# Sums of weight blocks made in DRAM: another order of copies and additions, and another place for a part of them

## The chip, the core and the metric

The kernel runs on one core of a Trainium2 chip. The core has five engines, each with an instruction queue of its own: PE (TensorE, matrix products; its weight loads are listed apart as PEld), DVE (VectorE), ACT (ScalarE), POOL (GpSimd) and SP (SyncE, which here only issues DMAs). DMAs are issued from the queues of SP, ACT and POOL. The metric is device time of the whole program in microseconds (us); lower is better. Times of several runs and one profiled execution are given.

## The reference

One inference step of a two-layer streaming encoder, for a prompt of 512 tokens and a running stream of 64 more, 576 columns in all, width 1024. Each layer is a token mixer (layer 0: causal pooling; layer 1: sparse attention with a rotary embedding, an indexer that picks 256 keys per token, and cached keys and values for the running stream) and a squared-ReLU MLP of width 4096, with residual adds and RMS norms:

```python
def _mlp(h, w_up, w_down):
    u = jax.nn.relu(h @ w_up)
    return (u * u) @ w_down

for i in range(DEPTH):
    h = _rmsnorm(x, norm_mix[i])
    ...
    x = x + y.astype(x.dtype)
    x = x + _mlp(_rmsnorm(x, norm_mlp[i]), mlp_w_up[i], mlp_w_down[i]).astype(x.dtype)
```

## The kernel before

**Products.** Activations lie transposed in SBUF, 128 features by 576 tokens. Every f32 weight block is split in two parts, an upper one that ACT casts (line 207) and a lower one, the difference that DVE or POOL makes (line 208), and PE multiplies three combinations. A weight block of 128 x 1024 is loaded into a tile `raw` by SP (the MLPs) or ACT (the attention), line 146. Blocks are made two ahead of PE (`next_block`).

**Fewer products.** Where two row blocks and two token halves meet, `Pair` (`DownPair`, `UpPair`) computes a 2 x 2 block product with seven products instead of eight (Strassen's scheme in Winograd's form). Besides the weights themselves it needs four sums of the weights' quarters a11, a12, a21, a22: s1 = a21 + a22, s3 = a21 + a11, s2 = s1 + a11, s4 = s2 + a12 (signs are taken care of elsewhere). In layer 0 the down products are pairs, and their sums are made in SBUF by POOL (lines 258 to 263, tile `sum`), from weights that SP loads. In layer 1 there are 24 pairs (12 up, 12 down), and their sums are made in DRAM ahead of time, in a tensor `mixed`: for each sum SP copies the first term into its place (line 218, 256 KB), and POOL then issues a DMA that adds the second term there (line 220). In the second MLP, SP loads `raw<-mixed` like any weight. So for one pair there are four copies and four additions, with a chain s1, s2, s4.

**Order.** `mixing` is a generator that issues a copy, yields, issues its addition, yields: eight steps a pair, pair after pair. In the first MLP each of the 16 calls of `up` takes seven steps (14 pairs, 56 sums), in the second each of the first 16 pairs takes five (10 pairs, 40 sums). A copy is placed behind the latest weight load of SP (`issue_after`). A scheduler then orders the instructions of each engine; the engine executes them in that order, so that whatever waits holds what stands behind it.

**The late attention.** `steps` runs over 40 units (one key group, two heads or a part of the running stream): scores on PE, softmax on DVE and ACT (line 1204), transposes, values, and from unit 18 on the output projection of the first 256 tokens (`wa`). Group by group, four units ahead, SP loads the queries (line 1279), and for the last four groups the cached keys (line 1084), which ACT casts and POOL subtracts (lines 286 and 287). POOL also makes index scores (lines 1171 and 1173) until the units of line 1225 with 384 columns begin.

Of the kernel before, what the change touches and what calls it, by code (L numbers as in the profile page):

```python
# [12 lines left out]
ALU = mybir.AluOpType  # L13
# [3 lines left out]
P = 128  # L17
# [26 lines left out]
AHEAD = 2  # L44
BLOCKS = 3
VS = 2
MIXES = (7, 5)


@with_exitstack  # L50
def pool_dsa_kernel(ctx: ExitStack, tc: tile.TileContext, a, o):
# [56 lines left out]
    def f32(t):  # L108
        return t.bitcast(F32)
# [100 lines left out]

    def mixing():

        for (kind, c, q), n in pairs.items():
            (a11, a12), (a21, a22) = ([r[:, i * 512:(i + 1) * 512] for i in range(2)] for r in rows(kind, 1, c, q))
            s1, s2, s3, s4 = (mixed[:, n, i] for i in range(4))
            for dst, src, add in ((s1, a21, a22), (s3, a21, a11), (s2, s1, a11), (s4, s2, a12)):
                with tc.issue_after(last_of["sync"].ins):
                    nc.sync.dma_start(dst, src)
                yield
                pool.dma_start(dst, add, accum_op=ALU.add)  # L220
                yield

    mixes = mixing()
# [259 lines left out]
    def mlp(layer, gi, strassen, order=range(KT), end=None):  # L483
# [165 lines left out]

        bx0 = norm.s2[:, :HT]  # L650

        def mix():
            for _ in range(MIXES[layer]):
                next(mixes, None)

        def up(c, q):
            if not layer:
                mix()
            if q >= PLAIN[layer][c]:
                mix()  # L660
                v = new_v()
                pair = UpPair(bx, seeded(), v)
                pair.opening()
                pair.closing()
                activated(v)
                finished(c, q, v)
                return
            first = (c, q) == (0, 0)
            pts = []
            if not layer and not first and not late:  # L670
                v = new_v()
                for i in range(2):
                    pt = up_plain(range(KT))
                    for h in range(2):
                        dve.scalar_tensor_tensor(v[:, 2 * i + h], pt[h][:, :HT], 0.0, halves(norm.rb)[:, h], ALU.max, ALU.mult)
                    act.activation(v[:, 2 * i:2 * i + 2], v[:, 2 * i:2 * i + 2], AF.Square)
                    if (c, q) == (3, 3):
                        us[c][q] = us[c][q] or u_tile()
                        factors_by_tile(i, v, us[c][q])
                if us[c][q] is None or q == 0:  # L680
                    finished(c, q, v)
                return
            for i in range(2):
                pts.append(up_plain(order if first else range(KT)))
                if late:
                    norm.spread()
                    v = new_v()
                    activated(v, late.pop())
                    finished(c, 0, v)
                if not first:  # L690
                    with tc.issue_after(last_of["diag"].ins), tc.issue_after(last_of["rt"].ins):
                        next(mixed, None)
            if first:
                norm.stats()
                late.append(pts)
                return
            v = new_v()
            activated(v, pts)
            finished(c, q, v)
# [4 lines left out]
        for c in range(4):  # L704
            for q in range(c > 0, 4):
                up(c, q)
            if c < 3:
                up(c + 1, 0)
            if c < strassen:
                for q in range(KT // 2):  # L710
                    if layer:
                        mix()
                    pair = DownPair(q, us[c], seeded(), layer > 0)
                    pair.opening(c == 3 and q == 0)
                    pair.closing((c, q) != (3, 3))
                continue
            phase["spare"] = room("bx", 7, "spare")[:7]
            for m in range(KT if end is None or c < 3 else KT - LAST):
                w = next_block()
                pt = [psum1("dn") for _ in range(2)]  # L720
                project(tuple(pt), w, us[c])
                for h in range(2):
                    d = halves(x[m])[:, h]
                    dve.tensor_tensor(d, d, pt[h][:, :HT], ALU.add)
# [302 lines left out]
    def attention(parts):  # L1027
# [244 lines left out]
        class Group:  # L1272
            def __init__(self, i, g):
# [2 lines left out]
                self.sums = small(n, f"sums{n}")  # L1276
                if i < 4:
                    self.q = slot("a", "q")[:, :4 * P].rearrange("p (h t) -> p h t", h=4)
                    nc.sync.dma_start(f32(self.q), qd[g][:, :, i * P:(i + 1) * P])
                else:  # L1280
                    self.q = slot("a", "q")[:, :4 * TS].rearrange("p (j t) -> p j t", j=2)
                    for j in range(2):
                        nc.sync.dma_start(f32(self.q[:, j].rearrange("p (h t) -> p h t", h=2)), qd[g][:, j::2, TP:T])
                    self.ck = split_cache(a["cache_k"][g], "ck", ks[g], pool)

            def normalise(self):
# [43 lines left out]
        def steps():  # L1330

            ranked = {0}
            for u in range(-4, total + 2):
# [18 lines left out]
                    units[u - 2].group.outputs()  # L1352
                if u >= 18 and u % 2 == 0:
                    next(first_out, None)
                yield

        def pace():
# [152 lines left out]
```

## Time and profile before

| | us |
|---|---|
| runs | 1166.62 median of 3 (1161.0 to 1167.46) |
| the profiled execution | 1167.88, its span 1166.0 |
| before and in the first MLP | 0 to 455 |
| first half of the attention, to the last index score on POOL | 455 to 619 |
| late attention and output projection | 619 to 741 |
| second MLP and end | 741 to 1166 |
| PE busy, share of the span | 1097.8 (94%) |

A row of the table of stretches has, for each engine, busy time and (x) instructions, then the granted TensorE clock, the share of time in which the 16 DMA engines were busy, and GB/s. A row of a timeline has start, length, engine, line, operation, out<-in, count, and in brackets the idle time before it and what ended it. SPq and POOLq are the queues of the engines that issue DMAs.

### The profile page before, as it was taken

Reading aid. Unit: us, or ns where it says so; the run is one execution under the profiler, and the core shown is the slowest. Engines: PE = TensorE matmul, PEld = TensorE weight load, DVE = VectorE, ACT = ScalarE, POOL = GpSimd, SP = SyncE. Lnnn points to the kernel's source line nnn. Section 1 sums busy time; section 2 is a strip of 40 time slices with the busy share of each in tenths; the row PEclk is TensorE's granted clock in tenths of the full one; section 3 lists DMA queues with packets and bytes.
Section 4 is the critical chain, followed back from the end, with each engine's and each line's share of the span. In section 5 each row is a group of like instructions: output and inputs, shape, how many; then the busy total and the mean of one; then the engine's idle time right before and its main releaser. Section 6 shows DMA issues by size and latency. Waiting matters only on the chain.

```text
span 1166.0 us, 20650 instructions
## 1 busy us (share of the span) xinstructions
PE 1097.8 (94%) x8118; PEld 1078.4 (92%) x8118; DVE 791.0 (68%) x1438; ACT 555.6 (48%) x925; POOL 310.8 (27%) x275
## 2 busy tenths in 40 slices
PE   8999999899789999999899999999999699899995
PEld 8998999899789999999889999999998699899995
DVE  7766657556556777659999944798657566765644
ACT  8443334334234445435388665566346335544531
POOL 3224423422441540047963440000111111000002
PEclk9999999999989999999989999999999899999998
DMA  6867368547735745357642341536888888745402
GB/s 215 191 180 149 94 186 194 112 141 174 161 91 153 179 127 179 107 136 212 182 125 65 116 142 48 172 104 179 231 237 245 220 225 254 216 137 177 140 19 82
DMA packets 81745, 183.54 MB, mean 157 GB/s; under 512 B 12289, under 2 KB 23856, under 8 KB 81648
## 3 DMA queue, kind: packets, MB, share of 16 engines
q1 hardware_dynamic: 63072, 139.71, 38.0%
q0 software_dynamic: 13824, 25.17, 14.2%
q10 hardware_dynamic: 4752, 17.34, 4.9%
q8 instruction: 64, 1.05, 0.4%
q14 instruction: 33, 0.27, 0.1%
HBM read 167.10 MB, written 61.22 MB: 196 GB/s over the span
## 4 chain that ended last, share of the span: by engine, by line
PE 46%; DVE 11%; DMA 9%; ACT 3%; issue 2%; POOL 1%; SPq 0%; DVEq 0%; ACTq 0%; POOLq 0%
PE seed L403 8%; PE up L557 6%; PE c L403 5%; PE a L403 5%; PE dn L300 4%; DMA mixed<-in_w_down 4%; PE pj L300 4%; DVE w L208 3%; PE o L1264 3%; PE wo L300 2%; PE wa L300 2%; DMA raw<-mixed 2%; DVE work L1189 2%; PE sc L1225 2%; DVE m L1188 1%
## 5 line engine op out<-in xcount | busy, mean ns | idle before, releaser
L207 ACT CAST w<-raw 128x1024 fp32r<-128x1024 f32 (+2 forms) x242 | 211.6, 889 | 274.8 <-PE seed L403 81.4
L208 DVE TENSOR_TENSOR w<-raw,w 128x1024 fp32r<-128x1024 f32 (+2 forms) x224 | 243.8, 1095 | 105.3 <-ACT w L207 104.2
L557 PE MATMUL up<-xs,w 128*128 128x288 f32 x1536 | 205.9, 295 | 0.5 <-ACT rbm L331 0.5
L557 PEld LDWEIGHTS up<-xs,w 128*128 128x128 f32 x1536 | 203.8, 188 | 0.9 <-ACT rbm L331 0.9
L403 PE MATMUL seed<-u,w 128*128 128x288 f32 x1008 | 150.2, 300 | 19.7 <-ACT seed L428 19.3
L403 PEld LDWEIGHTS seed<-u,w 128*128 128x128 f32 x1008 | 141.3, 192 | 21.7 <-ACT seed L428 21.1
L403 PE MATMUL a<-u,w 128*128 128x288 f32 x672 | 104.5, 302 | 6.9 <-ACT w L207 5.6
L220 POOL DMA_DIRECT2D mixed<-in_w_up x48 | 39.6, 851 | 259.2 <-DMA mixed<-mixed 140.4
L403 PE MATMUL c<-u,w 128*128 128x288 f32 x672 | 102.7, 298 | 3.0 <-ACT u L592 1.9
L403 PEld LDWEIGHTS a<-u,w 128*128 128x128 f32 x672 | 96.3, 194 | 8.5 <-ACT w L207 6.0
L403 PEld LDWEIGHTS c<-u,w 128*128 128x128 f32 x672 | 94.5, 190 | 4.4 <-ACT u L592 2.2
L300 PE MATMUL pj<-xs,w 128*128 128x288 f32 x672 | 93.0, 294 | 0.0
L220 POOL DMA_DIRECT2D mixed<-in_w_down x48 | 40.2, 894 | 192.0 <-DMA mixed<-mixed 155.9
L300 PEld LDWEIGHTS pj<-xs,w 128*128 128x128 f32 x672 | 90.5, 188 | 0.7
L403 PE MATMUL seed<-bx,w 128*128 128x288 f32 x432 | 65.7, 305 | 6.2 <-ACT seed L428 6.2
L208 DVE TENSOR_TENSOR w<-sum,w 128x1024 fp32r<-128x1024 f32 (+1 forms) x32 | 33.8, 1056 | 51.8 <-ACT w L207 51.6
L403 PEld LDWEIGHTS seed<-bx,w 128*128 128x128 f32 x432 | 61.7, 195 | 7.0 <-ACT seed L428 6.9
L207 ACT CAST w<-sum 128x1024 fp32r<-128x1024 f32 (+1 forms) x32 | 26.7, 834 | 72.4 <-POOL sum L263 63.4
L300 PE MATMUL dn<-u,w 128*128 128x288 f32 (+2 forms) x384 | 51.9, 295 | 1.0 <-ACT u L286 1.0
L300 PEld LDWEIGHTS dn<-u,w 128*128 128x128 f32 x384 | 51.0, 188 | 1.4 <-ACT u L286 1.2
L754 POOL TENSOR_TENSOR x<-x,spare 128x320 f32<-128x320 f32 (+1 forms) x9 | 8.1, 934 | 148.4 <-ACT spare L750 148.4
L1204 ACT ACTIVATE p<-p,nm 128x128 f32<-128x128 f32 (+4 forms) x72 | 41.9, 583 | 11.7 <-DVE nm L1203 11.1
(279 smaller groups left out, 1934.9 us busy)
## 6 DMA issues: line engine op xcount, KB each, us to landing
raw<-in_w_up SPq DMA_DIRECT2D x52, 512.0 KB, 4.3
raw<-in_w_down SPq DMA_DIRECT2D x52, 512.0 KB, 4.2
raw<-mixed SPq DMA_DIRECT2D x48, 512.0 KB, 5.3
mixed<-in_w_down POOLq DMA_DIRECT2D x48, 256.0 KB, 6.1
mixed<-mixed SPq DMA_DIRECT2D x48, 256.0 KB, 3.3
mixed<-in_w_up POOLq DMA_DIRECT2D x48, 256.0 KB, 5.7
raw<-in_w_o ACTq DMA_DIRECT2D x16, 512.0 KB, 4.1
raw<-in_w_in ACTq DMA_DIRECT2D x15, 512.0 KB, 4.3
```

Of the source, the lines that this page charges most:

```text
L207: act.copy(w[:, 0, at], src[:, at])
L208: how["sub"].tensor_tensor(w[:, 1, at], src[:, at], f32(w[:, 0, at]), ALU.subtract)
L220: pool.dma_start(dst, add, accum_op=ALU.add)
L300: pe.matmul(pt[h][:, :m] if isinstance(pt, tuple) else pt[:, h, :m], wt, xs[k][:, part, c:c + m], start=(k == 0 and i == 0), stop=(k == n ...
L403: pe.matmul(bank[:, :HT], wt[:, at], ut, start=first and j == 0 and i == 0, stop=j == 3 and i == 2, skip_group_check=True)
L557: pe.matmul(pt[h][:, :HT], w[:, wt, k * P:(k + 1) * P], moving(k, part, h), start=n == 0 and i == 0, stop=n == KT - 1 and i == 2)
L754: pool.tensor_tensor(x[k][:, t], x[k][:, t], rb, ALU.mult)
L1188: dve.max(m8[:np_], wk[:np_])
L1189: dve.match_replace(wk[:np_], m8[:np_], wk[:np_], TAKEN)
L1204: act.activation(dst, dst, AF.Exp, scale=-1.0, bias=nm, accum_out=sums)
L1225: pe.matmul(pt[:, hh, :nw], q[:, 2 * s + hh], ks[g][:, part, :nw], start=part == 0, stop=part == 1)
L1264: pe.matmul(oc[:, 2 * s + hh], pT[:, c:c + P], V[:, kt, vs], start=kt == 0, stop=kt == i)
```

## The change

The order of the sums is changed, and where the steps are taken; the sums, their number and the products stay. `mixing` now goes over all pairs n together: a step with the copies of s1 and s3 of pair n, then a step with the copies of s2 of pair n - 1 and s4 of pair n - 2; each step first issues the additions of the step before. That makes 28 x 2 = 56 steps for 24 pairs, the last four pairs' worth of which only drain. A step is taken by every call of `up` and every down pair of the first MLP (16 + 16 = 32 steps), by the units from 18 on of the attention (u = 18 to 41, 24 steps), and by the pairs of the second MLP. 32 and 24 are all 56, so that the calls in the second MLP find nothing left, although the change was described as reaching six of its pairs. The loads of queries set `last_of["sync"]`, so that a copy in the attention is placed behind the latest of them.

```diff
-MIXES = (7, 5)
...
     def mixing():
-        for (kind, c, q), n in pairs.items():
+        def parts(p):
+            kind, c, q = order[p]
             (a11, a12), (a21, a22) = ([r[:, i * 512:(i + 1) * 512] for i in range(2)] for r in rows(kind, 1, c, q))
-            s1, s2, s3, s4 = (mixed[:, n, i] for i in range(4))
-            for dst, src, add in ((s1, a21, a22), (s3, a21, a11), (s2, s1, a11), (s4, s2, a12)):
-                with tc.issue_after(last_of["sync"].ins):
-                    nc.sync.dma_start(dst, src)
-                yield
-                pool.dma_start(dst, add, accum_op=ALU.add)
+            s1, s2, s3, s4 = (mixed[:, p, i] for i in range(4))
+            return {"s1": (s1, a21, a22), "s3": (s3, a21, a11), "s2": (s2, s1, a11), "s4": (s4, s2, a12)}
+
+        order, copied = list(pairs), []
+        for n in range(len(order) + 4):
+            for step in (((n, "s1"), (n, "s3")), ((n - 1, "s2"), (n - 2, "s4"))):
+                for dst, add in copied:
+                    pool.dma_start(dst, add, accum_op=ALU.add)
+                copied.clear()
+                for p, name in step:
+                    if 0 <= p < len(order):
+                        dst, src, add = parts(p)[name]
+                        with tc.issue_after(last_of["sync"].ins):
+                            nc.sync.dma_start(dst, src)
+                        copied.append((dst, add))
                 yield
...
-        def mix():
-            for _ in range(MIXES[layer]):
+        def up(c, q):
+            if not layer or q >= PLAIN[layer][c]:
                 next(mixes, None)
-
-        def up(c, q):
-            if not layer:
-                mix()
             if q >= PLAIN[layer][c]:
-                mix()
                 v = new_v()
...
                 for q in range(KT // 2):
-                    if layer:
-                        mix()
+                    next(mixes, None)
                     pair = DownPair(q, us[c], seeded(), layer > 0)
...
-                    nc.sync.dma_start(f32(self.q), qd[g][:, :, i * P:(i + 1) * P])
+                    last_of["sync"] = nc.sync.dma_start(f32(self.q), qd[g][:, :, i * P:(i + 1) * P])
...
                 if u >= 18 and u % 2 == 0:
                     next(first_out, None)
+                if u >= 18:
+                    next(mixes, None)
                 yield
```

The queues, as the scheduler orders them. **POOL in the first MLP**, third group of down pairs (`sum` and `raw` are the pairs' sums and weights, `mixed` the additions). Before:

```order
L258 TENSOR_TENSOR sum_3225<-raw_3015 128x512
L220 DMA mixed<-in_w_down 128x512
L259 TENSOR_TENSOR sum_3225<-sum_3225,raw_3013 128x512
L261 TENSOR_TENSOR raw_3015<-raw_3015,raw_3013 128x512
L220 DMA mixed<-in_w_down 128x512 x2
L258 TENSOR_TENSOR sum_3416<-raw_3149 128x512
L220 DMA mixed<-in_w_down 128x512
L259 TENSOR_TENSOR sum_3416<-sum_3416,raw_3147 128x512
L261 TENSOR_TENSOR raw_3149<-raw_3149,raw_3147 128x512
L220 DMA mixed<-in_w_down 128x512 x3
L263 TENSOR_TENSOR sum_3225<-sum_3225,raw_3013 128x512
L258 TENSOR_TENSOR sum_3530<-raw_3414 128x512
```

The same place after the change:

```order
L267 TENSOR_TENSOR sum_3210<-raw_3006 128x512
L222 DMA mixed<-in_w_down 128x512
L268 TENSOR_TENSOR sum_3210<-sum_3210,raw_3004 128x512
L270 TENSOR_TENSOR raw_3006<-raw_3006,raw_3004 128x512
L222 DMA mixed<-in_w_up 128x512
L267 TENSOR_TENSOR sum_3405<-raw_3137 128x512
L222 DMA mixed<-in_w_down 128x512
L268 TENSOR_TENSOR sum_3405<-sum_3405,raw_3135 128x512
L270 TENSOR_TENSOR raw_3137<-raw_3137,raw_3135 128x512
L222 DMA mixed<-in_w_down 128x512 x3
L272 TENSOR_TENSOR sum_3210<-sum_3210,raw_3004 128x512
L267 TENSOR_TENSOR sum_3523<-raw_3403 128x512
```

Three additions still stand ahead of the first pair's last sum (now line 272), but they are an s3, an s2 and an s4 of three different pairs, where before they were links of one pair's chain; and additions now also stand among the sums that follow.

**SP in the late attention**, from the last query load with 128 tokens on (`x<-xd` is the residual stream read back). Before:

```order
L1279 DMA q_7339<-q_6141 128x4x128
L1392 DMA x_8017<-xd 128x1152
L1084 DMA raw_7455<-in_cache_k 128x512
L1283 DMA q_7450<-q_5683 128x2x64 x2
L1392 DMA x_8018<-xd 128x1152
L1084 DMA raw_7572<-in_cache_k 128x512
```

After:

```order
L1282 DMA q_7379<-q_6149 128x4x128
L228 DMA mixed<-in_w_up 128x512 x2
L228 DMA mixed<-mixed 128x512
L1397 DMA x_8097<-xd 128x1152
L228 DMA mixed<-mixed 128x512
L1087 DMA raw_7503<-in_cache_k 128x512
L1286 DMA q_7498<-q_5691 128x2x64 x2
L228 DMA mixed<-in_w_up 128x512 x2
L228 DMA mixed<-mixed 128x512
L1397 DMA x_8098<-xd 128x1152
L228 DMA mixed<-mixed 128x512
L1087 DMA raw_7628<-in_cache_k 128x512
```

Ahead of each load of cached keys (line 1087) there now stand four copies, of which two (`mixed<-mixed`) wait for an addition. All 35 copies left by the first MLP stand in this part of SP's queue, 34 of them ahead of the last load of cached keys.

**SP in the second MLP**, two down pairs. Before:

```order
L146 DMA raw_9279<-in_w_down 128x1024
L146 DMA raw_9281<-mixed 128x1024
L146 DMA raw_9283<-mixed 128x1024
L218 DMA mixed<-mixed 128x512
L146 DMA raw_9285<-in_w_down 128x512
L218 DMA mixed<-in_w_down 128x512 x2
L146 DMA raw_9397<-in_w_down 128x1024
```

After:

```order
L145 DMA raw_9344<-in_w_down 128x1024
L145 DMA raw_9346<-mixed 128x1024
L145 DMA raw_9348<-mixed 128x1024
L145 DMA raw_9350<-in_w_down 128x512
L145 DMA raw_9457<-in_w_down 128x1024
```

No copy stands between the weights there any more, nor anywhere else in the second MLP.

More of the change, by code (lines that the diff above doesn't have):

```diff
@@ L1282, in __init__ @@
                     for j in range(2):
-                        nc.sync.dma_start(f32(self.q[:, j].rearrange("p (h t) -> p h t", h=2)), qd[g][:, j::2, TP:T])
+                        last_of["sync"] = nc.sync.dma_start(f32(self.q[:, j].rearrange("p (h t) -> p h t", h=2)), qd[g][:, j::2, TP:T])
                     self.ck = split_cache(a["cache_k"][g], "ck", ks[g], pool)
```

## Prediction

> **What bounds the kernel now.** I read the page first (slices), then a table of stretches, then the waits of the two MLPs, then single waits in order of time.
>
> ```profile
> PE   8999999899789999999899999999999699899995
> DMA  6867368547735745357642341536888888745402
> ```
>
> A slice is 29.15 us. PE is nearly always busy, so the time is won or lost in the few thin slices: the 11th (291 to 321 us, first MLP), the 32nd (904 to 933) and the 35th (991 to 1020, both second MLP). The DMA row is at 7 or 8 from the 29th slice to the 35th, and low, 1 to 4, in the late attention (22nd to 25th, 612 to 729 us).
>
> ```profile
> core 0: us, PE busy (x) PEld busy (x) DVE busy (x) ACT busy (x) POOL busy (x), PEclk, DMA share, GB/s
> 100.00:120.00 20.00, 17.65 (x117) 16.48 (x116) 11.01 (x16) 6.28 (x8) 7.70 (x8) 0.91 0.63 127
> 200.00:220.00 20.00, 16.56 (x116) 16.32 (x115) 11.12 (x17) 6.54 (x9) 9.66 (x8) 0.93 0.68 162
> 300.00:340.00 40.00, 28.26 (x198) 28.02 (x197) 18.71 (x27) 9.84 (x13) 18.07 (x15) 0.83 0.58 125
> 617.00:694.00 77.00, 76.77 (x636) 74.83 (x635) 62.14 (x182) 52.93 (x127) 27.83 (x25) 1.00 0.33 96
> 850.00:1010.00 160.00, 141.05 (x991) 137.83 (x990) 102.71 (x138) 77.35 (x111) 22.86 (x28) 0.95 0.85 236
> 1010.00:1030.00 20.00, 17.62 (x126) 16.69 (x125) 15.62 (x21) 10.94 (x14) 0.00 (x0) 1.00 0.51 146
> 1030.00:1100.00 70.00, 70.00 (x527) 70.00 (x526) 44.38 (x59) 34.73 (x49) 0.00 (x0) 1.00 0.55 167
> ```
>
> I count matmuls rather than busy time, because a slow matmul is busy too. Undisturbed, 527 matmuls run in 70 us: 7.53 a us. By that rate the rows before fall short by 4.5 us (117 of 150.6), 4.6, 13.7, and for 850 to 1010 by 28.4 us (991 are 131.6 us of work). The late attention, 617 to 694, has full PE and a DMA share of 0.33.
>
> Why the first MLP loses: the waits of 60 to 460 us (who waited for whom, total, times, longest), and then SP, POOL and PE in order of time:
>
> ```profile
> POOL mixed L220 <- DMA mixed<-mixed: 144.8, 20, 15.1
> ...
> ACT w L207 <- POOL sum L263: 63.4, 15, 12.8
> ```
> ```profile
> 306.49 0.48 SPq L218 DMA_DIRECT2D mixed<-mixed  x1
> ...
> 314.59 0.48 SPq L218 DMA_DIRECT2D mixed<-mixed  x1
> ```
> ```profile
> 313.08 1.93 POOL L220 DMA_DIRECT2D mixed<-in_w_down  x2
> 320.16 0.81 POOL L220 DMA_DIRECT2D mixed<-in_w_down  x1 [5.15 <-DMA mixed<-mixed]
> 320.70 1.55 POOL L263 TENSOR_TENSOR sum<-sum,raw 128x512 f32<-128x512 f32 x1
> ```
> ```profile
> 325.43 3.25 PE L403 MATMUL seed<-u,w 128*128 128x288 f32 x12 [11.74 <-ACT seed L428]
> ```
>
> POOL's additions wait for copies, a copy s2 or s4 waits on SP for the addition before it (306.49, 314.59), and sum L263, which the next weight block needs, stands on POOL behind such an addition: it runs at 320.70, and ACT had waited up to 12.8 us for it. PE then idles 11.74 us.
>
> Why the second MLP loses: SP's own waits of 850 to 1010 us, and one case on SP and PE:
>
> ```profile
> SPq L218 <- DMA mixed<-in_w_down: 45.1, 6, 9.6
> SPq L218 <- DMA mixed<-in_w_up: 41.6, 6, 9.3
> ```
> ```profile
> 913.45 0.48 SPq L218 DMA_DIRECT2D mixed<-mixed  x1
> 914.03 0.53 SPq L146 DMA_DIRECT2D raw<-in_w_down  x1
> ```
> ```profile
> 921.84 0.85 PE L403 MATMUL a<-u,w 128*128 128x288 f32 x2 [4.71 <-ACT w L207]
> ```
>
> From 850 to 1010 SP stands 86.7 of 160 us at copies that wait for additions. One case: it is held at a copy until 913.45, only then issues the weights of 914.03, and PE waits 4.71 us for the block made of them. SP's queue, not the transfer alone, is the bound there.
>
> **The change part by part.** The sum is made against the profiled execution, 1167.88 us (span 1166.0 and 1.88 around it), 1.26 us over the median 1166.62 of the runs shown.
>
> *Nothing is saved in work:* 96 copies and 96 additions before and after; the counting of steps gives 61 of each in the first MLP where 56 stood, and the last 35 in the attention instead of 40 in the second MLP. No step of it is left for the second MLP.
>
> *First MLP.* The two-hop chain ahead of L263 goes. After the change three additions still stand ahead of the sum (order below the change), but s1, s3 and s2 wait for nothing recent, and s4 only for an s2 addition issued a step earlier; that is one hop, an addition and a copy (6.1 and 3.3 us, rows below), where 306.49 to 320.16 shows two, 13.7 us. One hop less is some 9 us earlier; of the 12.8 us that ACT waited at the worst place, up to 4 remain, and PE's 11.74 idle us began about a us after ACT's, so that 3 or so can remain. At 100 and 200 us the waits were half as long and vanish. Of 4.5 + 4.6 + 13.7 = 22.8 us I take 19 back, bounds 8 (POOL is held a hop in every group) and 23. New here: two copies and two additions beside each down pair, where none stood. An addition holds POOL some 0.8 us (313.08 has two in 1.93), against sums of 1.55 us; I cost it at nothing because the pairs' sums stand two blocks ahead of PE. If that cover is gone, it is the 8.
>
> *Second MLP.* All sums are gone from SP, and the stretch 850 to 1010 becomes like 1030 to 1100, which already runs without them: full rate at a DMA share of 0.55. One loss there is no DMA: where the third chunk passes from ups to downs (1010 to 1030, no sums in flight) 126 matmuls take 20 us, 3.3 us lost, and the like will stay at the second chunk. 28.4 - 3.3 = 25 us back, bounds 18 and 28.
>
> *Late attention.* Here 35 copies and 35 additions come into a stretch that lost nothing. The queues' shares of 750 to 1010 us (packets, MB, share), the page's issues (KB each, median us to landing), and POOL, ACT and PE in order of time:
>
> ```profile
> q1 hardware_dynamic: 16154, 43.83, 50.8%
> q0 software_dynamic: 5760, 10.49, 24.8%
> ```
> ```profile
> mixed<-in_w_down POOLq DMA_DIRECT2D x48, 256.0 KB, 6.1
> mixed<-mixed SPq DMA_DIRECT2D x48, 256.0 KB, 3.3
> ```
> ```profile
> 616.35 2.90 POOL L1173 TENSOR_TENSOR work<-work,rl 64x576 f32<-64x576 f32 x2
> ```
> ```profile
> 656.45 0.62 ACT L286 CAST ck<-raw 128x512 fp32r<-128x512 f32 x1 [1.65 <-DMA raw<-in_cache_k]
> ...
> 693.52 0.62 ACT L286 CAST ck<-raw 128x512 fp32r<-128x512 f32 x1
> 694.05 0.78 ACT L1204 ACTIVATE p<-p,nm 128x576 f32<-128x576 f32 x1
> ```
> ```profile
> 703.23 0.76 PE L1233 MATMUL sc<-ck,q 128*128 128x288 f32 x4
> ```
>
> Price of a sum in time of the 16 DMA engines, from the two queue rows (750 to 1010 us, 260 us): q0 holds 40 additions (10.49 MB by 0.262), 0.248 x 260 / 40 = 1.61 us each; q1 moves a MB in 0.508 x 260 / 43.83 = 3.01 us, so a copy of 0.262 MB is 0.79 us. SP's new order puts 34 of the copies, and so 32 additions that they or their successors wait for, ahead of the load of the last cached keys (raw<-in_cache_k). They can start when POOL is done with the index scores, at 619.25 (616.35 + 2.90). Work to be done before that load lands: 32 x 1.61 + 34 x 0.79 = 78.4 us, and what the stretch moves already, 0.33 x 77 = 25.4: together 103.8 us in the 74.3 us to 693.52, where ACT casts those keys. At full engines they land at about 723, 29.5 us late. ACT's order is fixed: behind the cast stands the softmax of 694.05, and the first keys' cast at 656.45 already waited 1.65 us for its load with a softmax behind it; so a late load holds all of ACT's queue. PE needs the cast keys at 703.23, 9.7 us after the cast, and half of that is work in between (POOL's difference, the softmax); I take 5 us as slack that ACT can lose. 25 us remain, spread over the four casts of cached keys. Bounds: nothing (all hidden) and 42 (the same work at the 0.85 share of the stretch 850 to 1010: 103.8 / 0.85 = 122, landing at 741, 48 late, less 5).
>
> The Trainium skill, "DMA: Bandwidth & Descriptors", section "Anatomy of one DMA — SWDGE (gpsimd) path", fits a DMA issued by GpSimd as 2.0 us plus bytes by 436 GB/s. By it an addition of 256 KB would hold the engines an estimated 0.6 us instead of the 1.61 of the trace, the work would be 32 x 0.6 + 26.9 + 25.4 = 72 us, and it would just fit: the attention would lose nothing. The trace has the price and decides; by the page the time would be that of the first rival.
>
> *Sum:* 1167.88 - 19 - 25 + 25 = 1148.9 in the profiled execution, 1147.6 by the median. I predict 1148.
>
> **The rivals.**
>
> *The attention hides the sums.* Its DMA row is 1 to 4 tenths, PE has 5 us of slack per cast, and the engines can be seen at more than full share for a while:
>
> ```profile
> 170.00:180.00 10.00, 10.00 (x78) 10.00 (x77) 6.79 (x11) 5.30 (x6) 3.21 (x4) 1.00 1.06 278
> ```
>
> Against it stands that 1.06 over the whole stretch still makes 98 us of 74. If the price of an addition alone on its engines is much under 1.61, it holds: 1167.9 - 44, 1124 (1123 by the median). Chance 0.15.
>
> *The attention is held as the second MLP was.* SP waits for additions, POOL for copies, and the engines are filled to 0.85 only: +42 instead of +25, 1166, no change. After the idle 11.74 us at 325.43 the first 12 matmuls took 3.25 us, where 12 take 1.59 at 7.53 a us. The Trainium skill, "TensorE: Matmul & The Clock Gate", Part 1, says that the array's clock is halved after an idle window of some 3.4 us and for about as long; the trace agrees (3.25 against 1.59), and by it four stalls of that length would add an estimated 1.7 us each, 1173 in this case. Chance 0.13.
>
> *Slower.* One mechanism: ACT's in-order wait at the four casts of cached keys. It decides when it costs more than the 44 us won, that is when the last keys land after 742 (693.5 + 44 + 5), the engines being filled under 0.84; at 0.78, landing at 752, the loss is 54 and the time 1177. For it: four hops (copy, addition, copy, addition) lie between loads, and SP has nothing else to issue meanwhile. Against it: two to three pairs are in flight at once, which is what the stagger does. Chance 0.09.
>
> *The change doesn't do what it says* in the first MLP: three additions still stand ahead of the sum, the wins there are 8 and the rest as forecast: 1160. Chance 0.08; my own forecast has the remaining 0.55.
>
> **How the numbers follow.** Likeliest 1148 (0.55, with its own range 1138 to 1160). The range reaches down to 1127, almost to the hidden case, and up to 1167, past the case without change: 0.8. A measurement of this kernel tells about 0.5% from no change, 5.8 us. Faster by more than that (under 1160.8): 0.15, 0.53 of the likeliest, half of the 0.08, and 0.03 of the held case, 0.75. Within: 0.02 + 0.04 + 0.08 of the held case + 0.02 of the slower one, 0.16. Slower: the rest of those two, 0.09. The range leaves out half of the hidden case (0.07) and, above, the slower one and the upper third of the held one (0.13).
>
> **What would show it.** First MLP: waits of ACT for the sum (63.4 us before) under 20, PE's 11.74 gone or under 4. Second MLP: no wait of SP at a copy, 850 to 1010 (shifted) at 7.4 matmuls a us or more. Attention: a DMA share of 0.9 or more from 620 on, waits of ACT for raw<-in_cache_k of 20 us or more in total (1.65 at the first keys before), the second MLP's first matmul 25 us late beside what the first MLP won. Wrong would be: the attention's share full and no wait of ACT (then the cover is larger than I read), or the second MLP still thin without sums (then its weights, not the sums, were late).

## The result

The change takes 1161.82 us (median of 20 runs, 1151.22 to 1169.82), the kernel before 1167.40 (median of 20, 1160.76 to 1171.48). The ratio is 0.9942, with a 95% interval of 0.9919 to 0.9965: faster by 5.6 us, where 19 were forecast. The ratio leaves out the slowest run of after, which counts as a slow one (without it the median is 1160.86). The profiled execution of after took 1165.96 us, its span 1164.2.

The slices of the page after the change, to be laid beside those of before:

```profile
PE   9999999999999989999797897999999999999995
PEclk9999999999999999999898995999999999999997
DMA  6346686586676674456559995243455555545402
```

The thin slices of both MLPs are gone (11th, 32nd, 35th before). New thin ones stand at the 22nd, 23rd and 25th (611 to 669 and 698 to 728 us), the late attention, and the last of them has a granted clock of 5 tenths. The table of stretches says the same in counts of matmuls (columns as before):

```profile
300.00:340.00 40.00, 39.04 (x290) 38.50 (x290) 26.29 (x38) 14.90 (x19) 18.57 (x18) 1.00 0.66 153
617.00:694.00 77.00, 66.07 (x517) 63.65 (x515) 49.32 (x137) 40.51 (x93) 43.66 (x47) 0.93 1.07 263
694.00:740.00 46.00, 39.28 (x217) 36.77 (x216) 10.98 (x32) 14.53 (x41) 10.12 (x11) 0.70 0.43 110
850.00:1010.00 160.00, 157.63 (x1165) 156.70 (x1164) 116.56 (x157) 87.46 (x122) 0.00 (x0) 0.99 0.53 158
```

From 300 to 340 us PE runs 290 matmuls (198 before), from 850 to 1010 it runs 1165 (991). From 617 to 694 it runs 517 (636), with the DMA engines full, and after that at a clock of 0.70. (The attention begins 12.9 us earlier after the change, at 442.1 us, so equal times are not quite equal work there; the table below is free of that.)

To put every kernel of this study on one scale, I cut each profiled execution at four matmuls: the first of the first MLP (`up`), the first of the attention (`pj`), the last of the output projection (`wo`) and the last of the second MLP (`dn`). In us:

| | first MLP | attention | second MLP |
|---|---|---|---|
| before | 418.1 | 285.7 | 410.2 |
| after | 406.1 (-12.0) | 318.4 (+32.7) | 387.7 (-22.5) |
| forecast | -19 | +25 | -25 |

The three differences and 0.8 us ahead of the first MLP make -2.6; the end takes 0.9 us longer, and the spans differ by 1.8. These are two single executions, as is every stretch given for the kernels below. That the medians lie 5.6 apart and not 2 is the spread between runs, of which more below: the profiled run of after is 4 us above its median.

### The profile page after: what moved, and what is told of

Its sections match the earlier page's. It is cut to its first block, busy times and chain, and to the rows that moved or that the text cites. A ratio compares the mean times of both kernels' runs of the same rounds, so it can differ in the third digit from the quotient of the medians.

```text
span 1164.2 us, 20675 instructions
## 1 busy us (share of the span) xinstructions
PE 1104.6 (95%) x8118; PEld 1086.0 (93%) x8118; DVE 808.9 (69%) x1438; ACT 555.6 (48%) x925; POOL 307.4 (26%) x275
## 4 chain that ended last, share of the span: by engine, by line
PE 53%; DVE 9%; DMA 9%; issue 3%; POOL 3%; ACT 3%; SPq 0%; DVEq 0%; ACTq 0%; POOLq 0%
PE seed L412 13%; PE c L412 8%; PE up L566 8%; PE a L412 8%; PE dn L309 4%; PE pj L309 3%; DVE w L207 2%; DMA mixed<-in_w_down 2%; DMA raw<-in_cache_k 2%; DMA raw<-in_w_down 2%; PE v L1061 1%; ACT w L206 1%; DVE work L1192 1%; DMA mixed<-mixed 1%; DVE m L1191 1%
## 5 line engine op out<-in xcount | busy, mean ns | idle before, releaser
L412 PEld LDWEIGHTS seed<-u,w 128*128 128x128 f32 x1008 | 138.9, 188 | 11.9 <-ACT seed L437 5.3
L267 POOL TENSOR_TENSOR sum<-raw 128x512 f32<-128x512 f32 x16 | 24.9, 1556 | 152.7 <-DMA raw<-in_w_down 145.0
L207 DVE TENSOR_TENSOR w<-sum,w 128x1024 fp32r<-128x1024 f32 (+1 forms) x32 | 42.0, 1313 | 29.7 <-ACT w L206 29.7
L412 PE MATMUL seed<-bx,w 128*128 128x288 f32 x432 | 62.5, 296 | 0.0
L412 PEld LDWEIGHTS seed<-bx,w 128*128 128x128 f32 x432 | 59.3, 188 | 0.1
L222 POOL DMA_DIRECT2D mixed<-in_w_up x48 | 43.6, 1012 | 40.2 <-DMA mixed<-mixed 21.9
L206 ACT CAST w<-sum 128x1024 fp32r<-128x1024 f32 (+1 forms) x32 | 26.6, 833 | 48.3 <-POOL sum L272 41.1
```

What stands on the lines that cost most here:

```text
L206: act.copy(w[:, 0, at], src[:, at])
L207: how["sub"].tensor_tensor(w[:, 1, at], src[:, at], f32(w[:, 0, at]), ALU.subtract)
L267: pool.tensor_tensor(s[:, :512], r2[:, :512], r2[:, 512:], ALU.add)
L412: pe.matmul(bank[:, :HT], wt[:, at], ut, start=first and j == 0 and i == 0, stop=j == 3 and i == 2, skip_group_check=True)
```

## Where the attention's 32.7 us are

PE's idle times there, what SP, POOL and ACT waited for from 600 to 745 us (total, times, longest), and the two DMA queues from 620 to 700 us (packets, MB, share):

```profile
631.44 1.33 PE L1248 MATMUL pt<-ident,p 128*128 128x128 f32 x5 [7.67 <-ACT p L1207]
...
664.28 0.33 PE L1248 MATMUL pt<-ident,p 128*128 128x128 f32 x1 [2.88 <-ACT p L1207]
...
699.62 0.79 PE L1236 MATMUL sc<-ck,q 128*128 128x288 f32 x4
...
707.51 0.69 PE L1303 MATMUL ot<-ident,on 128*128 128x128 f32 x2 [6.49 <-DVE wo L1323]
...
710.05 1.31 PE L1236 MATMUL sc<-ck,q 128*128 128x288 f32 x4
```
```profile
SPq L228 <- DMA mixed<-in_w_up: 32.8, 8, 8.8
SPq L228 <- DMA mixed<-in_w_down: 29.9, 8, 6.5
```
```profile
POOL mixed L222 <- DMA mixed<-mixed: 25.4, 10, 5.6
POOL mixed L222 <- DMA mixed<-in_w_down: 12.6, 5, 4.3
```
```profile
ACT ck L295 <- DMA raw<-in_cache_k: 16.3, 3, 6.0
...
ACT ot L1310 <- POOL w L207: 8.5, 1, 8.5
```
```profile
q0 software_dynamic: 4074, 7.41, 54.7%
q1 hardware_dynamic: 8551, 11.02, 42.0%
```

PE stands idle 7.67 + 2.88 + 6.49 = 17.0 us. The second and the third of these stand behind cached keys that ACT waits for (casts at 660.52 and 705.55). The first does not: ACT waits there for POOL, whose difference of output weights stands behind two additions that wait for copies:

```profile
622.35 0.81 POOL L222 DMA_DIRECT2D mixed<-in_w_down  x1 [1.57 <-DMA mixed<-mixed]
626.63 0.81 POOL L222 DMA_DIRECT2D mixed<-in_w_up  x1 [3.47 <-DMA mixed<-mixed]
627.17 2.76 POOL L207 TENSOR_TENSOR w<-raw,w 128x512 fp32r<-128x512 f32 x2
```
```profile
630.35 0.43 ACT L1310 CAST ot<-ot 128x128 fp32r<-128x128 f32 x2 [8.52 <-POOL w L207]
```

The rest is the clock: four `sc` matmuls take 0.79 us at 699 and 1.31 at 710, and the trace has the clock at half from 703 to 730 us. From the `ot` transposes of 707.51 to the last `wo` matmul PE needs 53.0 us, where before it needed 42.2 for the same work: 10.8 us in this window alone. Two shorter windows (6.8 us at 628, 3.4 at 666) belong to the other two idle times; they and small gaps are the 4.9 us that are left of the 32.7.

Three things could have made these idle times: the time of the DMA engines (share 1.07), SP's queue (copies wait for additions, cached keys behind them), or POOL's queue (additions wait for copies, differences of weights behind them, as in the 8.52 us above). The experiments take them apart in part.

## The experiments

Times are medians, each with its ratio to the kernel before as run beside it on the same chip.

**No sums in the attention.** In none_in_attention the two lines of the units go, and in the second MLP each pair takes two steps:

```diff
                 if u >= 18 and u % 2 == 0:
                     next(first_out, None)
-                if u >= 18:
-                    next(mixes, None)
                 yield
```

> The units of the attention take no step; each of the first pairs of the second MLP takes two instead, so all sums that the first MLP leaves are made there, in the staggered order. The attention should get back all of the 32.4 us that it lost against the kernel before, by any theory (a rest of over 5 us would mean that something else than the sums slowed it). What the second MLP then costs tells the two theories of its old loss apart. If the time of the DMA engines sets it: 35 sums x 2.4 us = 84 us of transfers in some 120 us that are already filled to 0.55, 84 against 54 free, so 10 to 25 us lost, 1145 to 1155. If the chain of waits on SP set it (copy waits for the addition just before it), the stagger has removed it, and under 6 us are lost: 1130 to 1137.

1139.56 us, 0.9754 (0.972 to 0.9789). The attention takes 286.8 us, 1.1 over before, so the sums are all of its loss. The second MLP takes 397.3, 9.6 over after, at a DMA share of 0.97 where the sums are made:

```profile
780.00:860.00 80.00, 75.40 (x554) 73.97 (x553) 51.98 (x75) 35.87 (x48) 16.43 (x20) 1.00 0.97 268
```

The median lies between the two ranges; the loss of 9.6 is by the lower edge of what the engines' time asked for. But the chain of waits isn't gone at this pace: from 735 to 1000 us SP still stands 46.7 us at copies that wait for additions, so this run doesn't tell the two theories apart.

**One step a pair.** one_per_pair is the same with the attention's lines gone and nothing else changed, so that each pair of the second MLP takes one step.

> No step in the attention; each pair of the second MLP takes one step (21 calls until the sums are done) where none_in_attention took two (12 calls) and lost 9.7 us there beside 0.97 of the DMA engines' time. Theory of the engines' time: 84 us of transfers spread over some 210 us that are filled to 0.55, 94 us free, so the share stays under 0.95 and the second MLP loses under 4 us: 1131 to 1136. Rival: a sum costs about 0.28 us wherever it stands, by its place in SP's and POOL's queues, and nothing changes: 1138 to 1142.

1130.30 us, 0.9673 (0.964 to 0.9706). The attention takes 285.7, the second MLP 385.7: no more than with no sums in it at all (387.7 after). This is the stretch in which the sums are made:

```profile
770.00:970.00 200.00, 197.15 (x1468) 195.78 (x1467) 148.79 (x208) 107.60 (x145) 26.23 (x32) 1.00 0.85 236
```

1468 matmuls in 200 us are 7.34 a us, at a DMA share of 0.85. Before, the same share of 0.85 stood beside 6.2 (991 in 160 us). So at 0.85 it was not the share that thinned the second MLP, but the waiting of SP, which from 740 to 970 us of this run doesn't wait for an addition at all. Spread over 21 calls, 35 sums cost nothing there.

**The old chain at these places.** In chained the generator of before issues its steps at nearly the same places: four at each call of the first MLP, five at each pair of the second, none in the attention.

> The order of before, pair after pair and each sum behind the one before, at places like those of one_per_pair: four of its steps (two sums) at each `up` and each down pair of the first MLP, 64 sums in all, five at each pair of the second MLP as before, none in the attention. Theory that the stagger makes the gain: the first MLP falls behind by 13 us or more at 316 us and the second loses 20 to 28 us as before, 1160 to 1170. Rival, that the places make it (fewer sums in one call, fewer left for the second MLP): the first MLP keeps over 12 of its 18 us, the second loses under 18, 1142 to 1155.

1164.83 us, 0.9978 (0.9953 to 1.0003): no faster than before. The first MLP takes 421.0, the second 403.8, against 408.4 and 385.7 for one_per_pair. The waits of chained are of the kind of before, of ACT from 60 to 460 us and SP from 840 to 1000 us:

```profile
ACT w L206 <- POOL sum L262: 53.3, 14, 8.6
```
```profile
SPq L217 <- DMA mixed<-in_w_up: 49.5, 7, 10.1
SPq L217 <- DMA mixed<-in_w_down: 19.7, 3, 7.2
```

In the first MLP, with nearly the same places, the stagger is worth 12.6 us here, and 10 to 19 against the ten kernels that have the staggered first MLP of after (402.0 to 410.9). (The expected place did not hold: from 300 to 340 us chained runs 259 matmuls, between 198 before and 290 after; it loses the rest elsewhere.) In the second MLP the 18.1 us are not the stagger's alone, since the places differ: chained issues its 32 copies within 179 us, one_per_pair its 35 within 233. none_in_attention, staggered and denser still (35 within 127), takes 397.3, so the stagger is worth at least 6.5 us of the 18.1, and what the wider spacing adds was not tried apart. The new places alone gain 3 us at the median, within the noise: 6.4 less in the second MLP, 2.9 more in the first.

**Fewer in the attention.** every_second_unit halves the attention's steps; the rest goes to the second MLP.

```diff
-                if u >= 18:
+                if u >= 18 and u % 2 == 0:
                     next(mixes, None)
```

> Steps at every second unit of the attention (12 instead of 24), the other 12 at the first pairs of the second MLP. Theory of the engines' time: the attention has 17 additions x 1.61 + 18 copies x 0.79 + 25.4 = 67 us of transfers ahead of the last cached keys, under the 74 that it has, so it loses under 4 us; the second MLP's 17 sums, 41 us, fit in what is free there; 1130 to 1138. Rival, the order of the queues (SP's copies wait for additions, POOL's additions for copies, loads and differences stand behind them): each step costs as much as before, half the steps lose half, 14 to 18 us in the attention, and 1144 to 1150.

1146.42 us, 0.9806 (0.9766 to 0.9846), by the number that the rival gave: the attention loses 15.8. But not for its reason alone: from the `ot` transposes on, PE needs 52.6 us for what takes 42.2, so 10.4 of the 15.8 are one window at half clock (17.1 us from 695.7) and the idle of only 2.34 us that it follows:

```profile
617.00:694.00 77.00, 71.86 (x580) 68.33 (x578) 51.56 (x143) 44.93 (x104) 43.16 (x44) 1.00 0.90 220
694.00:728.00 34.00, 32.82 (x180) 30.97 (x181) 10.33 (x32) 14.07 (x39) 3.04 (x4) 0.75 0.35 92
```

**The chain taken away, the transfers kept.**

```diff
-"s2": (s2, s1, a11), "s4": (s4, s2, a12)}
+"s2": (s2, s1 if p < 13 else a22, a11), "s4": (s4, s2 if p < 13 else a21, a12)}
```

> For the pairs whose second and fourth sums are made in the attention (from the 14th on), their copies take a quarter of the weights as source and not the sum before, so no copy waits for an addition; number, size and place of all copies and additions stay. These sums are then not those of the reference. Theory of the engines' time: nothing changes in the attention, it loses 28 to 36 us against the kernel before, DMA share 1.05 from 620 to 700 us as before; 1157 to 1166. Rival, the order of the queues: SP's waits at copies (62.7 us from 600 to 745) go, the cached keys are loaded when they are wanted, and the attention loses under 12 us; 1135 to 1145.

1161.49 us, 0.9946 (0.9918 to 0.9974); the attention takes 318.8, as after. SP's waits at copies for additions fall from 62.7 us to 2.2:

```profile
SPq L228 <- DMA mixed<-in_w_down: 1.7, 2, 1.0
SPq L228 <- DMA mixed<-in_w_up: 0.5, 1, 0.5
```

and nothing is gained. SP's waiting for additions is not what costs the attention its time. (In its place SP waits 20.9 us for POOL's differences before it loads cached keys, 3.5 in after.) The DMA share from 620 to 700 us stays at 1.04.

**POOL's waits shortened.** In two_behind an addition is issued two steps behind its copy:

```diff
-            for step in (((n, "s1"), (n, "s3")), ((n - 1, "s2"), (n - 2, "s4"))):
-                for dst, add in copied:
+            for step in (((n, "s1"), (n, "s3")), ((n - 1, "s2"), (n - 3, "s4"))):
+                for dst, add in waiting:
                     pool.dma_start(dst, add, accum_op=ALU.add)
-                copied.clear()
+                waiting, copied = copied, []
```

> The change as it is, with additions issued two steps behind their copies and the fourth sum one pair later; the attention still takes 24 steps. Theory that a good part of the attention's 32.7 us comes from POOL (its additions wait 43 us there for copies that have just been issued, and the differences of weights and keys stand behind them): these waits fall under 15 us, the attention loses 14 to 22 us, 1144 to 1152. Theory of the engines' time: the same transfers in the same stretch, nothing changes, the attention loses 28 to 35 us, 1157 to 1164.

1161.21 us, 0.9937 (0.9912 to 0.9962). The attention takes 312.9, a loss of 27.2 between the two theories' ranges and near that of the engines, where the median lies too. POOL's waits did not fall under 15 us: 20.0 + 8.9 + 6.1 remain, since copies land late. So it is a weak test of POOL's part.

**Half the bytes.** In half_rows the copies and additions of the attention move 64 rows.

```diff
                         dst, src, add = parts(p)[name]
+                        if n >= 16:
+                            dst, src, add = dst[:64], src[:64], add[:64]
...
-                    m = mixed[:, pairs[tuple(srcs)]]
+                    m = mixed[:, pairs[tuple(srcs)] % 14]
```

> The change as it is, but every copy and addition that is issued in the attention moves 64 rows and not 128; their number, order and waits stay. The second MLP reads the sums of other pairs in place of those that are half made, the same bytes, so its output is not the reference's. Theory of the engines' time: 32 x 0.8 + 34 x 0.4 + 25.4 = 65 us of transfers ahead of the last cached keys in the 74 there are; the attention loses under 6 us of its 32.7: 1132 to 1138. Rival, it is the number of transfers and their waits on SP and POOL: 28 to 33 lost, 1157 to 1163. Between them: 10 to 16 lost as with every_second_unit, which moved about the same bytes (then a total that fits is not enough, since loads stand behind bursts): 1142 to 1148.

1142.73 us, 0.9781 (0.9738 to 0.9823). The attention loses 14.2 and not 32.7, at a share of 0.80; ACT waits for no cached key any more, and after the `ot` transposes the clock is full (42.4 us). With the same number of transfers and the same chains, 18.5 us go with the bytes, 10.6 of them in the stretch behind the `ot` transposes, where the clock stays full. Smaller transfers also land sooner: SP's waits at copies fall from 62.7 us to 22.0 and POOL's at additions from 43.1 to 21.4, so the engines' time and these waits fall together. The 14 that stay are the third answer of the expectation; whether bursts or POOL's queue hold them (ACT waits 6.5 us for a difference of POOL's there) is open.

**The two queues relieved.** In keys_on_act ACT issues the cached keys; in differences_on_dve DVE makes the differences that stood behind POOL's additions; keys_and_differences does both.

```diff
-            nc.sync.dma_start(raw[:, :TP], src)
+            (act if s == "ck" else nc.sync).dma_start(raw[:, :TP], src)
...
-                    self.ck = split_cache(a["cache_k"][g], "ck", ks[g], pool)
+                    self.ck = split_cache(a["cache_k"][g], "ck", ks[g])
...
-next_block(sub=pool)
+next_block()
```

> The change as it is, but the four loads of cached keys are issued by ACT, so that they no longer stand behind copies in SP's queue. Theory of the queue's order: ACT's waits for these keys (16.3 us) fall under 6 and the attention loses 12 to 20 us, not 32.7: 1142 to 1150. Theory of the engines' time: the engines are full from 620 to 700 us whatever the queue, the keys or something else that is loaded there (weights, residual) come as late as before, 27 to 34 us lost: 1156 to 1164.

> The change as it is, but the differences of output weights and cached keys in the late attention are made by DVE and not by POOL, so that nothing that ACT or PE waits for stands behind POOL's additions there. If POOL's queue carries the part of the attention's 32.7 us that is left when the keys come early (20.0 in keys_on_act), this alone takes 8 to 14 us: 1148 to 1154, and the first idle of PE there (7.67 us at 631) goes; the last one, for the keys, stays. Rival, DVE (62 of 77 us busy there before) has no room and becomes what is waited for, or the engines are late anyway: 30 us lost or more, 1159 to 1168.

> Both together: cached keys issued by ACT and differences by DVE. If the two queues carry the loss and the engines' time is no bound by itself, the attention loses under 10 us of its 32.7, 1134 to 1142. If the DMA engines' time bounds it (share 1.05 from 620 to 700), whatever is loaded there comes late: 17 us or more are lost, 1147 to 1158.

keys_on_act: 1153.11 us, 0.9897 (0.9854 to 0.9941), the attention loses 20.0, between the two expectations. ACT's waits for the keys fall from 16.3 to 6.7, and the long window at half clock is gone (42.4 us from the `ot` transposes), but ACT's waits for POOL's differences grow from 10.5 to 22.8. differences_on_dve: 1155.44, 0.9906 (0.9871 to 0.994); the attention loses 26.0, again between the two: the first idle of PE goes as said, but the first keys are now waited for 15.6 us in one piece. keys_and_differences: 1152.00, 0.9844 (0.9811 to 0.9878); the attention loses 21.6, no less than with the keys alone. With both queues relieved the engines are as full as ever, and ACT waits somewhere else: 5.8 and 6.4 us ahead of two of its own loads (output weights issued at 637.41, cached keys at 655.07), by its rows until copies of sums have landed:

```profile
620.00:700.00 80.00, 68.30 (x523) 65.31 (x522) 56.70 (x147) 40.71 (x93) 25.43 (x31) 0.91 1.06 259
```
```profile
ACT pT L1249 <- DMA mixed<-mixed: 6.4, 1, 6.4
ACT ot L1310 <- DMA mixed<-mixed: 5.8, 1, 5.8
```

The result of the pair is what the engines' theory forecast: 20 us or more of the 32.7 stayed in each of the three, and a wait that is taken away comes back in another place. It does not show that theory by itself, since ACT still waits for transfers that land late, and half_rows shortens such waits too. Of the 12.7 us that keys_on_act wins, 10.6 are the stretch behind the `ot` transposes: the place of the keys in SP's queue decides over them by where the last idle falls.

**The clock by itself.** In filled_last 50 transposes of a constant stand on PE ahead of the two `ot` transposes of the last idle time.

```diff
                 tr = psum1("ot")
+                for _ in range(50 if (i, g) == (3, 3) else 0):
+                    pe.transpose(tr[:, :P], ident, ident)
```

> 50 transposes of a constant (5.5 us) are put on PE ahead of the two transposes that waited 6.49 us for the last cached keys; they are overwritten, the result stays. Theory that half of the attention's loss is the half clock granted after a wait (27.3 us of it from 703 to 730): the idle goes to 1 us or so, the clock stays full there, 9 to 12 us are gained, mean clock up by 0.010; 1150 to 1154. Rival, the clock is low there for another reason (the few matmuls of this place, or the waits before): window stays, 1160 to 1166.

1160.55 us, 0.9927 (0.9904 to 0.9951), in the range of the rival: the forecast gain did not come, though its reason is in the trace. The filling waited like the `ot` transposes themselves, and ran behind the idle time, not in it:

```profile
708.99 7.22 PE L1303 MATMUL ot<-ident 128*128 128x128 f32 x50 [2.42 <-DVE wo L1325]
716.05 0.38 PE L1305 MATMUL ot<-ident,on 128*128 128x128 f32 x2
...
717.41 0.78 PE L1236 MATMUL sc<-ck,q 128*128 128x288 f32 x4
```

Behind it the clock is full again (four `sc` in 0.78), and the rest takes 42.2 us as in an undisturbed run, where after needed 53.0: the 10.8 us are the clock's. The filling cost 7.2 of them, and in this execution a further idle of 3.39 us at 679 and a longer half-clock window at 627 took the rest.

**Steps at the ups alone.** ups_one_per_pair is one_per_pair with two steps at each `up` of the first MLP and none at the down pairs.

> As one_per_pair, and in the first MLP each `up` takes two steps and the down pairs none, the same 32 steps. The first MLP after the change lost 6.1 us anew (at 340, 395 and 425 us of its trace), where the sums of down pairs and additions stand together on POOL. If the additions beside the down pairs cause that, these 6 us go and the rest of the first MLP's gain stays: 4 to 7 us under one_per_pair. Rival: two steps at each `up` bring back what the change removed, since twice as many copies and additions stand together there: 5 to 18 us over one_per_pair, with waits of ACT for the sum of 30 us or more.

1128.14 us, 0.9661 (0.9632 to 0.969). The first MLP takes 402.5. In the ten other kernels with steps at every call and one step's lag it takes 402.0 to 410.9, so this is not told apart from one_per_pair, as the two intervals say too. Waits of ACT for the sum are 51.6 us, which did not bring the losses back. It and one_per_pair are the fastest of this study, some 3% under the kernel before.

## Why the prediction was right or wrong

**First MLP, -19 forecast, -12.0 measured.** The mechanism holds at the first and the third of the places named, which lose next to nothing any more (149 matmuls from 100 to 120 us, 290 from 300 to 340); the second still loses (125 from 200 to 220, with an idle of 1.83 us and a clock of 0.91). Matmul by matmul the three give back 3.5 + 0.6 + 13.9 = 18.0 us. ACT's waits for the sum fell less than I asked, to 41.1 us and not under 20, but the longest from 12.8 to 6.4, which PE's lead covers:

```profile
ACT w L206 <- POOL sum L272: 41.1, 14, 6.4
```

The term is too large by what I costed at nothing: at 340, 395 and 425 us of the new trace 6.1 us are lost anew. The largest of them, DVE and POOL in order of time and PE:

```profile
416.97 6.29 DVE L327 TENSOR_TENSOR s<-s,sq 128x576 f32<-128x576 f32 x1
423.18 0.44 DVE L469 TENSOR_TENSOR x<-x,c 128x288 f32<-128x288 f32 x1
...
426.13 0.75 DVE L327 TENSOR_TENSOR s<-s,sq 128x576 f32<-128x576 f32 x1
```
```profile
416.94 1.54 POOL L268 TENSOR_TENSOR sum<-sum,raw 128x512 f32<-128x512 f32 x1
418.19 1.54 POOL L270 TENSOR_TENSOR raw<-raw,raw 128x512 f32<-128x512 f32 x1
419.42 1.93 POOL L222 DMA_DIRECT2D mixed<-in_w_up  x2
420.51 2.12 POOL L272 TENSOR_TENSOR sum<-sum,raw 128x512 f32<-128x512 f32 x1
```
```profile
425.63 1.73 PE L412 MATMUL seed<-u,w 128*128 128x288 f32 x10 [4.04 <-DVE x L469]
```

An addition of DVE that takes 0.75 us takes 6.29 here, just as long as POOL's sums and additions follow one another, and PE waits 4.04 us for the DVE instruction behind it. In four of the ten kernels with this first MLP the same instruction takes 6.27 to 6.31 us, in the other six 0.75; their first MLPs take 405.6 to 410.9 and 402.0 to 407.6 us. So this loss is partly a matter of chance, and the -12.0 is one draw: in none of the ten does the first MLP win the 19 forecast. The Trainium skill, "SBUF — State Buffer", section "SBUF: two separate sides", says that VectorE with two inputs in SBUF and GpSimd share a port pair that one of them holds for a whole instruction while the other is blocked; the trace agrees, in that DVE's time ends within a us of POOL's last sum. That this is the cause was not tried by itself: ups_one_per_pair, which takes the additions away from the down pairs, lies within the spread of the others (the instruction takes 1.84 us there, as in before).

**Second MLP, -25 forecast, -22.5 measured.** Right: no wait of SP at a copy, 1165 matmuls in 160 us (7.3 a us; 7.4 was asked for).

**Late attention, +25 forecast, +32.7 measured.** This is the step that failed. The direction was right; the term is too small because it put the clock behind an idle PE at nothing, and it knew one path, late cached keys, where a second cost nearly as much idle time. The prices of the transfers held: 7.41 MB are 28.3 additions, 0.547 x 80 / 28.3 = 1.55 us each (1.61 forecast), and q1 moved a MB in 0.420 x 80 / 11.02 = 3.05 us (3.01). By the fit in the Trainium skill, "DMA: Bandwidth & Descriptors", section "Anatomy of one DMA — SWDGE (gpsimd) path", that the prediction weighed (an estimated 0.6 us), the attention would have lost nothing; the trace stands by 1.55. The last cached keys were cast 263.4 us after the attention's first matmul where they had been 238.5 after it: 24.9 us late (29.5 forecast). That these two lie close is partly luck: by 672 us PE was 14.9 us behind already, by two idle times and their clock, and SP's loads wait for PE too (10.9 us at the queries). PE stood idle 17.0 us, less than my 25, and only 9.4 of them by the path of the forecast; the first 7.67 came through POOL's queue, whose additions wait for copies, which the term did not have. What was missing is the clock: each idle time is followed by matmuls at half speed, the last by 23 us of them. In the last stretch this cost 10.8 us (53.0 against 42.2), and with the two shorter windows and small gaps it makes up the 15.7 us beside the idle time. I had put the clock into a rival at 1.7 us a stall and left it out of my own sum. ACT's waits for the keys are 16.3 us, where I asked for 20.

**The sum.** -19 became -12.0, +25 became +32.7, -25 became -22.5: 17 us of the forecast gain of 19 are gone in this pair of executions (13 at the medians). The three errors point the same way, and two of them are 7.0 and 7.7 us on terms of 19 and 25, while the forecast itself was their small difference.

**The rivals.** That the attention hides the sums (0.15) is wrong. The measured 32.7 lies midway between my own +25 and the +42 of the attention held at a share of 0.85 (0.13), but not by that mechanism: the engines were at 1.07, and the clock and POOL's queue made the difference. That three additions ahead of the sum leave the first MLP unimproved (0.08) is wrong; chained shows that it was the chain, not the count. The slower case (0.09) needed the last keys after 742 us; they were cast at 705.6 (718.5 counted as in before, with the 12.9 us that the attention begins earlier), and the four hops that I counted for it carry nothing, since without them (unchained) the loss is the same.

**What runs differ by.** The 20 runs of after lie between 1151.22 us at a mean granted clock of 0.982 and 1169.82 at 0.971, and the lower the clock, the longer the run in the main. A hundredth of mean clock is 23 us at half, and 11.6 us of work lost; the spread is the size of one such window more or less. That it is the window of the attention was not seen, since one run was profiled.

## What to carry to other kernels

A chain of transfers on two queues is best issued so that each link is a step older than what waits for it. The same sums at nearly the same pace, chained and staggered, differ by 30.7 us over both MLPs, a part of it by the wider spacing in the second, and the number of transfers did not have to fall for it. Where work is moved to fill a stretch that looks empty, add up the time of the DMA engines in that stretch first, and the cost of an idle PE with its clock: here 25 us of transfers stood there already and 78 were added in 74, while the same sums cost nothing in the second MLP at one step a pair. Such a total tells that time is lost, but not by which queue's wait. When the forecast is a small difference of large terms, its error is that of the terms.

## What the runs showed of the hardware

The clock came back far later in one place than in the others. In all fourteen traces I cut time into the 3.41 us pieces by which the clock record moves. Of 58 pieces at full clock with PE busy for under 0.4 of them, all were followed by half clock; of 44 with 0.4 to 0.6, 24; of 4337 with 0.7 or more, 12. An idle of 2.3 us is enough if it falls within one piece (every_second_unit, 2.34 us, then half clock from 695.7). The way back: of 109 pieces at half clock with PE busy for 0.9 or more, 87 were followed by full clock and 22 were not. Those from 707 to 727 us of after are among these: PE is busy, with `o` of 64 columns, `pt` of 128 and `sc` of 288; it ends about where `wo` with 320 columns begins, and so it does in every_second_unit, unchained and two_behind. In filled_last 50 transposes of 128 columns in a row bring the full clock back after one piece (708.8 to 712.2 us), and then the same stretch runs at full clock throughout. So it isn't 128 columns by themselves that hold the clock down; what in this stretch does was not tried apart. The Trainium skill, "TensorE: Matmul & The Clock Gate", Part 1, gives about 3.4 us of idle for the loss and one busy window of that length for the return; the trace agrees with the window, not with the need for a whole idle one, nor with one busy window for the return in this stretch.
